# Outputs in the place of inverses, an earlier first state, and a store ahead of the offsets: a chunked RWKV recurrence on one core

## The chip, the cores and the metric

The kernel runs on one core of a Trainium2 chip. The core has five engines that run their own instruction streams and meet through semaphores: TensorE (PE, matrix products; PEld is its weight load), VectorE (DVE), ScalarE (ACT, functions such as exp and ln), GpSimd (POOL) and SyncE (SP), and sixteen DMA engines that move data between the memory of the chip and the on-chip memories: SBUF, and PSUM, where TensorE writes its results. The metric is the time of one execution on the device, in microseconds (us).

## The reference

The reference is the WKV recurrence of RWKV: for each of 16 batches and each of 256 channels a running, exponentially decaying weighted mean of v with weights exp(k), kept stable by a running maximum. k and v have the shape 16 x 2048 x 256 in float32, w and u have 256 elements.

```python
for b in range(batch):
    aa, bb, pp = 0, 0, -1e38                    # per channel
    for t in range(seq_len):
        kk, vv = k[b, t], v[b, t]
        ww = u + kk
        qq = np.maximum(pp, ww)
        e1, e2 = np.exp(pp - qq), np.exp(ww - qq)
        output[b, t] = (e1 * aa + e2 * vv) / (e1 * bb + e2 + 1e-08)
        ww = pp - w + kk
        qq = np.maximum(ww, kk)
        e1, e2 = np.exp(ww - qq), np.exp(kk - qq)
        aa, bb, pp = e1 * aa + e2 * vv, e1 * bb + e2, qq
```

The decay carries the key with it: the new exponent is pp - w + kk, so the exponents are running sums over time, which the kernel builds with triangular matrices.

## The kernel before

Time is cut into 16 chunks of 128 steps, and the 16 batches into 4 groups of 4. A tile is one chunk of one group: 128 time steps (on the partitions) by 4 batches by 256 channels, 512 KB in float32. There are 64 tiles of k and 64 of v, and tile n is group n % 4 of chunk n // 4. The main loop handles one tile of k and v in each pass (a slot, numbered n), and the output of tile q = n - 9 nine slots later (`LAG`), because the state that enters a chunk must first be known. Ten more slots drain the last outputs.

For each tile:

- `round_k`: DVE rounds k for TensorE; `logs`: PE builds the logarithms of the weights in PSUM; `exps`: ACT takes the exponential of both kinds of weights (EZ) in bf16; `cast_v`: v to bf16 (some tiles of v are cast by the transfer itself); `times_v`: DVE multiplies the weights by v.
- `sums`: PE sums the weights, and the weights times v, over half chunks, for the state.
- `den`, `recip`: PE sums the denominators in PSUM, ACT makes their inverse as exp(-ln(x)) in an SBUF tile rd; `num`, `mult`: PE sums the numerators, DVE multiplies them by the inverse; `store`.

```python
    kpool = ctx.enter_context(tc.tile_pool(name="kpool", bufs=AHEAD))      # AHEAD = 6
    vpool = ctx.enter_context(tc.tile_pool(name="vpool", bufs=6))
    vbpool = ctx.enter_context(tc.tile_pool(name="vbpool", bufs=4))
    rpool = ctx.enter_context(tc.tile_pool(name="rpool", bufs=2))
    opool = ctx.enter_context(tc.tile_pool(name="opool", bufs=3))
...
    def recip(n, between=lambda: None):
        rd = rpool.tile([128, 2, D], F32, tag="rd", name="rd")
        for i in (slice(0, 1), slice(1, 2)) if n == NP - 1 else (slice(0, 2),):
            K(SC.activation(rd[:, i, :], DENB[:, i, :], ACT.Ln, scale=RS))
            between()
            K(SC.activation(rd[:, i, :], rd[:, i, :], ACT.Exp, scale=-1.0))
        RD[n] = rd
...
    def mult(n, bank, i):
        if n not in OT:
            OT[n] = opool.tile([128, 4, Dm], F32, tag="ot", name="ot")
        o, rd = OT[n].rearrange("p (i n) d -> p i (n d)", i=2), RD[n]
        K(DVE.tensor_mul(o[:, i, :], bank, rd[:, i, :]))

    def store(n):
        RD.pop(n)
        K(POOL.dma_start(out=rows_of(out, n), in_=OT.pop(n)))
```

Once for each chunk c there is a chain of small operations on the state, spread over the slots after the chunk's last tile by a plan. It ends with four transfers from SP (`inject`) that write the state into a row of the weights, where the denominators and numerators pick it up:

```python
    def state_frames(c):
        E = DVE if c in (0, NST - 1) else POOL
        LL, F = LL_of[c % 2], F_of[c % 2]
        for h, x in enumerate((LL_of[(c + 1) % 2][:, 1, :, 2:3], LL[:, 1, :, 1:2])):
            K(E.tensor_tensor(F[:, :, 1 + h:2 + h], x, LL[:, 1, :, 1 + h:2 + h], ALU.add))
...
    def state_scan(c):
        flat = [x.rearrange("p m s -> p (m s)") for x in (P_of[c % 2], F_of[c % 2], LL_of[c % 2][:, 0])]
        K(DVE.tensor_tensor_scan(*flat, 0.0, ALU.add, ALU.max))

    def state_offsets(c):
        E = DVE if c in (0, NST - 1) else POOL
        A, P, F = [x[c % 2] for x in (A_of, P_of, F_of)]
        Q = tiny.tile([128, 32, 2], F32, tag="Q", name="Q")
        K(E.tensor_tensor(Q, P[:, :, 0:2], F[:, :, 1:3], ALU.add))
        out = A.rearrange("p h m -> p m h")
        K(E.tensor_tensor(out[:, :, 0:2], Q, P[:, :, 1:3], ALU.subtract))
        K(E.tensor_single_scalar(out[:, :, 2:4], Q, CAP, op=ALU.min))
        K(E.tensor_single_scalar(out[:, :, 4:6], P[:, :, 1:3], -1.0, op=ALU.mult))
        K(E.tensor_copy(LL_of[(c + 1) % 2][:, 0, :, 0:1], P[:, :, 2:3]))
...
    def inject(c):
        cb = small.tile([128, 128], BF16, tag="cb", name="cb")
        K(DVE.tensor_copy(cb, st.pop((c, "CT"))))
    ...                                   # four transfers from SP into EZR
...
    later = {}
    for c in range(NST):
        s = 4 * c + 3
        plan = [(s + 1, "act", copy_sums), (s + 1, "pe", turn),
                (s + 2, "act", state_logs), (s + 2, "mid", state_frames), (s + 2, "chain", state_scan), (s + 2, "chain", state_offsets),
                (s + 3, "act", state_weights), (s + 3, "chain", state_chain),
                (s + 4, "nums", turn_back), (s + 4, "mid", inject), (s + 4, "mid", state_next)]
        if c == NST - 1:
            plan = [(s + 1, "copy", copy_sums), (s + 1, "turn", turn),
                    (s + 1, "recip", state_logs), (s + 1, "mid", state_frames), (s + 1, "mid", state_scan), (s + 1, "mid", state_offsets),
                    (s + 2, "recip", state_weights), (s + 2, "mid", state_chain),
                    (s + 3, "turn", turn_back), (s + 3, "first", inject)]
        for slot, where, f in plan:
            later.setdefault((slot, where), []).append((f, c))
```

The loops (the first nine slots, the main slots, the drain):

```python
    for n in range(LAG):

        load(n + AHEAD)
        exps(n)
        logs(n + 1)
        if n and n % 4 == 0:
            sums(n - 1)
        small_work(n, "act")
        small_work(n, "nums")
        if n % 4:
            sums(n - 1)
        small_work(n, "pe")
        idle_matmuls(4, NUMB)
        times_v(n)
        cast_v(n + 1)
        round_k(n + 2)
        small_work(n, "mid")
        small_work(n, "chain")
...
    for n in range(LAG, NP):

        q, qp = n - LAG, n - LAG - 1
        if n + AHEAD < NP:
            load(n + AHEAD)
        first = n == LAG
        if not first:
            num(qp, NUMB, 0)
            den(q)
        if n % 4 == 0:
            sums(n - 1)
        small_work(n, "nums")
        exps(n)
        small_work(n, "act")
        if not first:
            recip(q)
            mult(qp, NUMB, 0)
        small_work(n, "mid")
        if n + 2 < NP:
            round_k(n + 2)
        if n + 1 < NP:
            cast_v(n + 1)
        else:
            times_v(n)
        if not first:
            num(qp, NUMB, 1)
            mult(qp, NUMB, 1)
        small_work(n, "chain")
        if not first:
            store(qp)
        if n + 1 < NP:
            times_v(n)
            logs(n + 1)
        else:
            den(q + 1)
...
    sums(NP - 1)
    small_work(NP, "copy")
    for n in range(NP, NP + LAG + 1):

        q, qp = n - LAG, n - LAG - 1
        H = PS[:, 2 * (n % 2):2 * (n % 2) + 2, :]
        for i in range(2):
            num(qp, H[:, i, :], i)
        small_work(n, "turn")
        small_work(n, "first")
        if q < NP:
            recip(q, lambda: small_work(n, "recip"))
        if q + 1 < NP:
            den(q + 1)
        if qp == NP - 1:
            last_outputs(qp, H)
        else:
            mult(qp, H, slice(0, 2))
            store(qp)
        small_work(n, "mid")
        small_work(n, "pe")
        small_work(n, "last")
    assert not later
```

## Time and profile before

The median of three runs is 308.87 us (308.04 to 309.64). The profiled execution has a span of 307.7 us and a mean granted TensorE clock of 0.991.

| what | value |
|---|---|
| POOL busy | 220.5 us (72%), of which 150 us are the issue of transfers |
| read from HBM, written to HBM | 67.12 MB, 33.55 MB: 327 GB/s over the span |
| issue to landing, median: k, v, v cast to bf16 | 9.4, 9.8, 10.0 us |
| issue to landing, median: outputs, injected states | 8.1, 6.2 us |
| DVE, costliest groups | output multiplication 85.9 us, times v 78.1, rounding of k 48.5, cast of v 40.3 |
| ACT, costliest groups | exponentials of the weights 102.3 + 17.4 us, logarithm and exponential of the inverse 65.3 + 68.0 |
| first and last start of the big exponential (slots 9 and 63) | 38.2 and 275.8 us |

The page of a profile gives each engine's busy time and share of the span, then the span in 40 equal slices (each digit is the busy share in tenths), the DMA queues, the chain of work that ended last, the costliest groups of instructions with what ended the idle time ahead of them, and the transfers. Further views list who waited for whom (`A <- B: us in total, times, longest`) and the instructions of an engine in order of time: start, duration, engine, line, operation, tile written <- tile read, and in brackets the idle time before it and what ended it. Matmuls are pipelined, so a busy PE is not PE at its peak. Line numbers such as L198 are those of the kernel before.

### The profile page before, as it was taken

What the parts mean: (1) busy time and instruction counts of PE and PEld (TensorE: products, weight loads), DVE (VectorE), ACT (ScalarE), POOL (GpSimd) and SP (SyncE); (2) the same over time, 40 slices, a digit from 0 to 9 for tenths busy, and PEclk for the clock granted to TensorE, in tenths of its full rate; (3) what the DMA queues carried; (4) which work ended last, traced back from release to release, by engine and by line L of the source; (5) the groups of instructions that cost most, each with busy time, mean ns of one, the idle gap of its engine ahead of it and who ended that gap; (6) DMA issues with size and microseconds to landing.
All of it is one profiled execution on the core that took longest, in us unless ns stands there. A gap on an engine that the chain in (4) does not pass through costs nothing.

```text
span 307.7 us, 4967 instructions
## 1 busy us (share of the span) xinstructions
PE 274.2 (89%) x1716; PEld 126.6 (41%) x1716; DVE 263.4 (86%) x436; ACT 258.4 (84%) x251; POOL 220.5 (72%) x337
## 2 busy tenths in 40 slices
...
DMA  6999999999999999999989999999999999424676
GB/s 198 349 347 349 334 343 340 366 299 335 367 373 365 280 364 356 363 363 380 305 254 361 360 367 342 349 369 315 361 342 361 360 378 364 153 94 153 215 245 205
DMA packets 37339, 97.86 MB, mean 318 GB/s; under 512 B 6198, under 2 KB 14914, under 8 KB 37314
## 3 DMA queue, kind: packets, MB, share of 16 engines
...
q14 instruction: 12, 0.10, 0.1%
HBM read 67.12 MB, written 33.55 MB: 327 GB/s over the span
## 4 chain that ended last, share of the span: by engine, by line
DMA 27%; DVE 23%; PE 18%; POOL 11%; ACT 10%; issue 8%; DVEq 0%; SPq 0%; POOLq 0%; ACTq 0%
DMA out_dram<-ot 20%; DVE ot L359 7%; PE PS L185 5%; DVE km L171 5%; ACT EZR L198 4%; DMA EZR<-cb 4%; PE PS L353 4%; PE PS L340 4%; ACT rd L346 4%; DVE vb L211 4%; DVE EZR L216 3%; POOL Q L281 3%; DMA kr<-in_k_dram 2%; POOL A L285 2%; PE PS L180 2%
## 5 line engine op out<-in xcount | busy, mean ns | idle before, releaser
L359 DVE TENSOR_TENSOR ot<-PS,rd 128x512 f32<-128x512 f32 (+1 forms) x119 | 85.9, 723 | 24.8 <-PE PS L353 10.1
L198 ACT ACTIVATE EZR<-PS 128x2048 bf16<-128x2048 f32 x55 | 102.3, 1861 | 4.0 <-PE PS L185 3.7
L363 POOL DMA_DIRECT2D out_dram<-ot x63 | 49.5, 786 | 52.7 <-DVE ot L359 50.5
L216 DVE TENSOR_TENSOR EZR<-EZR,vb 128x2048 bf16<-128x2048 bf16 x64 | 78.1, 1220 | 2.3 <-ACT EZR L196 1.8
L346 ACT ACTIVATE rd<-PS 128x1024 f32<-128x1024 f32 (+1 forms) x65 | 65.3, 1005 | 5.6 <-PE PS L340 4.1
L348 ACT ACTIVATE rd<-rd 128x1024 f32<-128x1024 f32 (+1 forms) x65 | 68.0, 1046 | 2.0
L353 PE MATMUL PS<-EZR,LN 128*128 128x512 bf16 x128 | 49.0, 383 | 9.2 <-DVE ot L359 8.9
L63 POOL DMA_DIRECT2D kr<-in_k_dram x63 | 48.6, 772 | 5.9 <-DVE vb L211 2.9
L171 DVE CAST km<-kr 128x1024 fp32r<-128x1024 f32 x64 | 48.5, 757 | 3.4 <-DMA kr<-in_k_dram 3.4
L185 PE MATMUL PS<-km,NLE 128*128 128x512 f32 x128 | 47.4, 452 | 2.3 <-DVE km L171 2.2
L353 PE MATMUL PS<-EZR,IdN 128*128 128x512 bf16 x128 | 48.6, 379 | 0.0
L340 PE MATMUL PS<-EZR,L 128*128 128x512 bf16 x128 | 38.0, 379 | 6.6 <-ACT rd L346 4.0
...
L211 DVE CAST vb<-vr 128x1024 bf16<-128x1024 f32 x50 | 40.3, 805 | 1.3 <-DMA vr<-in_v_dram 1.3
L185 PE MATMUL PS<-km,NLZ 128*128 128x512 f32 x128 | 40.5, 398 | 0.0
L340 PE MATMUL PS<-EZR,Id 128*128 128x512 bf16 x128 | 38.0, 379 | 0.0
L180 PE MATMUL PS<-WU,CO 32*128 32x512 f32 x256 | 33.2, 500 | 3.8 <-ACT EZR L198 3.6
L240 PE MATMUL PS<-EZR,OH 128*32 128x256 bf16 x512 | 25.7, 279 | 1.4 <-DVE tb L299 0.4
L185 PEld LDWEIGHTS PS<-km,NLE 128*128 128x128 f32 x128 | 19.2, 189 | 18.5 <-issue 14.4
L185 PEld LDWEIGHTS PS<-km,NLZ 128*128 128x128 f32 x128 | 24.3, 190 | 5.8
L180 PEld LDWEIGHTS PS<-WU,CO 32*128 32x128 f32 x256 | 12.5, 183 | 32.2 <-ACT EZR L198 17.2
L196 ACT ACTIVATE EZR<-PS 128x1024 bf16<-128x1024 f32 x18 | 17.4, 1020 | 9.9 <-PE PS L185 9.9
...
## 6 DMA issues: line engine op xcount, KB each, us to landing
...
vb<-in_v_dram POOLq DMA_DIRECT2D x14, 256.0 KB, 10.0
EZR<-cb SPq DMA_DIRECT2D x64, 8.0 KB, 6.2
...
```

The source lines that it names most:

```text
L171: K(DVE.tensor_copy(km, kr_of.pop(n)))
L180: K(PE.matmul(half(n, q)[:, i, :], CO[g:g + 32, :], WU[g:g + 32, :], start=True, stop=False, tile_position=(g, 0), skip_group_check=True))
L185: K(PE.matmul(half(n, q)[:, i, :], (NLE, NLZ)[q], km[:, i, :], start=False, stop=True, skip_group_check=True))
L198: K(SC.activation(ez(n)[:, 0:2], PS[:, 0:4, :].rearrange("p (q i) x -> p q i x", q=2), ACT.Exp))
L211: K(DVE.tensor_copy(vb, vr))
L216: K(DVE.tensor_mul(ez(n)[:, 2:4], ez(n)[:, 0:2], vb.unsqueeze(1).broadcast_to([128, 2, 2, D])))
L340: K(PE.matmul(DENB[:, i, :], mats[m], ez(n)[:, q, i, :], start=q == 0, stop=q == 1, skip_group_check=True))
L346: K(SC.activation(rd[:, i, :], DENB[:, i, :], ACT.Ln, scale=RS))
L348: K(SC.activation(rd[:, i, :], rd[:, i, :], ACT.Exp, scale=-1.0))
L353: K(PE.matmul(bank, mats[m], ez(n)[:, q, i, :], start=q == 2, stop=q == 3, skip_group_check=True))
L359: K(DVE.tensor_mul(o[:, i, :], bank, rd[:, i, :]))
L363: K(POOL.dma_start(out=rows_of(out, n), in_=OT.pop(n)))
```

## The change

The change has five parts.

1. **Outputs in the place of inverses.** The multiplication writes its product over the inverse in rd, and the store reads rd. The pool of outputs is gone, rd has six buffers, and v in float32 has five in place of six. It is meant to give a store more time before its buffer is needed again.
2. **Store ahead of the offsets.** In the slot with the scan, POOL issues the store of the slot before it computes the state's offsets, and not after.
3. **Weights amid an inverse.** The state weights G = exp(A) are placed between the logarithm and the exponential of an inverse, and not ahead of both, so that the offsets have longer to come. In the drain the small logs and weights go behind the inverse.
4. **Loads.** SP loads k0, k1 and v0; k is loaded one tile ahead of v in the first slots; the zeros of `wuf` are written by DVE.
5. **An early first state chain.** For chunk 0 the chain is drawn together into two slots, v5 is cast on ACT, and the frames and offsets of chunk 1 run on DVE (as those of chunks 0 and 15 do). The idle products at the start are 12 in place of 16.

The diff (empty lines are cut, marked by dots where more than one):

```diff
--- before.py
+++ after.py
@@ -37,13 +37,13 @@
     LAG = 9
     RS = 2.0 ** -20
     CAP = 54.0
+    ON_DVE = (0, 1, NST - 1)
 
     consts = ctx.enter_context(tc.tile_pool(name="consts", bufs=1))
     kpool = ctx.enter_context(tc.tile_pool(name="kpool", bufs=AHEAD))
-    vpool = ctx.enter_context(tc.tile_pool(name="vpool", bufs=6))
+    vpool = ctx.enter_context(tc.tile_pool(name="vpool", bufs=5))
     vbpool = ctx.enter_context(tc.tile_pool(name="vbpool", bufs=4))
-    rpool = ctx.enter_context(tc.tile_pool(name="rpool", bufs=2))
-    opool = ctx.enter_context(tc.tile_pool(name="opool", bufs=3))
+    rpool = ctx.enter_context(tc.tile_pool(name="rpool", bufs=6))
     small = ctx.enter_context(tc.tile_pool(name="small", bufs=2))
     tiny = ctx.enter_context(tc.tile_pool(name="tiny", bufs=1))
     ps = ctx.enter_context(tc.tile_pool(name="ps", bufs=1, space=bass.MemoryType.PSUM))
@@ -52,7 +52,7 @@
     kr_of, vr_of, VB = {}, {}, {}
 
     def v_mode(n):
-        return "dma" if n >= 9 and n % 4 == 2 else "dve"
+        return "dma" if n >= 9 and n % 4 == 2 else "act" if n in (5,) else "dve"
 
     def rows_of(x, n):
         c, p = divmod(n, 4)
@@ -98,13 +98,14 @@
         K(eng.dma_start(out=wuf.rearrange("(g r) n d -> r g n d", r=32)[r, g0:4], in_=bass.AP(
             tensor=x.tensor, offset=x.offset, ap=[[0, 4 - g0], [0, 2], list(x.ap[0])])))
 
-    K(POOL.memset(wuf, 0.0))
+    fill(wuf, 0.0)
     fill(M1, -1.0)
     fill(I1, 0.0)
     load_k(0, SP)
+    load_k(1, SP)
+    load_v(0, SP)
     load_row(SC, 0, 0, w)
     load_row(SC, 1, 2, u)
-    load_v(0, SC)
     K(SC.preload_act_table_set("natural_log_exp_and_others"))
     fill(idle, 0.0)
     select(M1, GE, 0.0, -1, -1, [[1, 128]])
@@ -114,8 +115,8 @@
                     allow_small_or_imprecise_dtypes=True))
     for g in (2, 3):
         select(COf, NE, 1.0, -32 * g - 1, 1, [[0, 128]])
-    for n in range(1, 3):
-        load(n)
+    load_k(2)
+    load_v(1)

     NLE, NLZ, CO = matrix("NLE", F32R), matrix("NLZ", F32R), matrix("CO", F32R)
@@ -138,7 +139,8 @@
         for h in range(2):
             select(Sel[:, j, h], NE, 1.0, -r - h, 1, [[-16, 2], [-2, 4], [-32, 2]])
     for n in range(3, AHEAD):
-        load(n)
+        load_k(n)
+        load_v(n - 1)
     WU = consts.tile([128, D], F32R, tag="WU", name="WU")
     mats = {"OH": OH, "Sel": Sel.rearrange("p a h n c i -> p (a h) n (c i)")}
 
@@ -265,7 +267,7 @@
 
 
     def state_frames(c):
-        E = DVE if c in (0, NST - 1) else POOL
+        E = DVE if c in ON_DVE else POOL
         LL, F = LL_of[c % 2], F_of[c % 2]
         for h, x in enumerate((LL_of[(c + 1) % 2][:, 1, :, 2:3], LL[:, 1, :, 1:2])):
             K(E.tensor_tensor(F[:, :, 1 + h:2 + h], x, LL[:, 1, :, 1 + h:2 + h], ALU.add))
@@ -274,12 +276,13 @@
...
     def state_offsets(c):
-        E = DVE if c in (0, NST - 1) else POOL
+        E = DVE if c in ON_DVE else POOL
         A, P, F = [x[c % 2] for x in (A_of, P_of, F_of)]
+        out = A.rearrange("p h m -> p m h")
         Q = tiny.tile([128, 32, 2], F32, tag="Q", name="Q")
         K(E.tensor_tensor(Q, P[:, :, 0:2], F[:, :, 1:3], ALU.add))
-        out = A.rearrange("p h m -> p m h")
         K(E.tensor_tensor(out[:, :, 0:2], Q, P[:, :, 1:3], ALU.subtract))
         K(E.tensor_single_scalar(out[:, :, 2:4], Q, CAP, op=ALU.min))
         K(E.tensor_single_scalar(out[:, :, 4:6], P[:, :, 1:3], -1.0, op=ALU.mult))
@@ -332,7 +335,7 @@
                     in_=cb[x:x + 32, :]))
 
 
-    RD, OT = {}, {}
+    RD = {}
 
     def den(n):
         for m, q in (("L", 0), ("Id", 1)):
@@ -353,14 +356,11 @@
             K(PE.matmul(bank, mats[m], ez(n)[:, q, i, :], start=q == 2, stop=q == 3, skip_group_check=True))
 
     def mult(n, bank, i):
-        if n not in OT:
-            OT[n] = opool.tile([128, 4, Dm], F32, tag="ot", name="ot")
-        o, rd = OT[n].rearrange("p (i n) d -> p i (n d)", i=2), RD[n]
-        K(DVE.tensor_mul(o[:, i, :], bank, rd[:, i, :]))
+        rd = RD[n]
+        K(DVE.tensor_mul(rd[:, i, :], bank, rd[:, i, :]))
 
     def store(n):
-        RD.pop(n)
-        K(POOL.dma_start(out=rows_of(out, n), in_=OT.pop(n)))
+        K(POOL.dma_start(out=rows_of(out, n), in_=RD.pop(n).rearrange("p i (n d) -> p (i n) d", n=2)))
 
     def last_outputs(n, H):
         c, p = divmod(n, 4)
@@ -368,19 +368,24 @@
             mult(n, H[:, i, :], i)
             for j, eng in ((0, SP), (1, SC)):
                 b = 4 * p + 2 * i + j
-                K(eng.dma_start(out=out[b, c * TC:(c + 1) * TC, :], in_=OT[n][:, 2 * i + j, :]))
+                K(eng.dma_start(out=out[b, c * TC:(c + 1) * TC, :], in_=RD[n][:, i, Dm * j:Dm * j + Dm]))
 
     later = {}
     for c in range(NST):
         s = 4 * c + 3
         plan = [(s + 1, "act", copy_sums), (s + 1, "pe", turn),
-                (s + 2, "act", state_logs), (s + 2, "mid", state_frames), (s + 2, "chain", state_scan), (s + 2, "chain", state_offsets),
-                (s + 3, "act", state_weights), (s + 3, "chain", state_chain),
+                (s + 2, "act", state_logs), (s + 2, "mid", state_frames), (s + 2, "chain", state_scan), (s + 2, "store", state_offsets),
+                (s + 3, "recip", state_weights), (s + 3, "chain", state_chain),
                 (s + 4, "nums", turn_back), (s + 4, "mid", inject), (s + 4, "mid", state_next)]
+        if c == 0:
+            plan = [(s + 1, "act", copy_sums), (s + 1, "pe", turn), (s + 1, "round", state_logs),
+                    (s + 1, "round", state_frames), (s + 1, "round", state_scan), (s + 1, "round", state_offsets),
+                    (s + 2, "act", state_weights), (s + 2, "chain", state_chain), (s + 2, "chain", turn_back),
+                    (s + 2, "round", inject), (s + 2, "round", state_next)]
         if c == NST - 1:
             plan = [(s + 1, "copy", copy_sums), (s + 1, "turn", turn),
-                    (s + 1, "recip", state_logs), (s + 1, "mid", state_frames), (s + 1, "mid", state_scan), (s + 1, "mid", state_offsets),
-                    (s + 2, "recip", state_weights), (s + 2, "mid", state_chain),
+                    (s + 1, "post", state_logs), (s + 1, "mid", state_frames), (s + 1, "mid", state_scan), (s + 1, "mid", state_offsets),
+                    (s + 2, "post", state_weights), (s + 2, "first", state_chain),
                     (s + 3, "turn", turn_back), (s + 3, "first", inject)]
         for slot, where, f in plan:
             later.setdefault((slot, where), []).append((f, c))
@@ -393,33 +398,37 @@
         for _ in range(n):
             K(PE.matmul(bank, idle[:, 0:128], idle, start=True, stop=True, skip_group_check=True))
 
-    idle_matmuls(16, MISC)
+    idle_matmuls(12, MISC)
     round_k(0)
     K(DVE.tensor_copy(WU, wuf.rearrange("p n d -> p (n d)")))
     logs(0)
+    round_k(1)
     cast_v(0)
-    round_k(1)
     state_start()
     for n in range(LAG):
 
-        load(n + AHEAD)
+        load_v(n + AHEAD - 1)
+        load_k(n + AHEAD)
         exps(n)
-        logs(n + 1)
-        if n and n % 4 == 0:
+        if n % 4 == 0 and n:
             sums(n - 1)
         small_work(n, "act")
-        small_work(n, "nums")
+        if v_mode(n + 1) == "act":
+            cast_v(n + 1)
+        logs(n + 1)
         if n % 4:
             sums(n - 1)
         small_work(n, "pe")
         idle_matmuls(4, NUMB)
         times_v(n)
-        cast_v(n + 1)
+        small_work(n, "chain")
         round_k(n + 2)
-        small_work(n, "mid")
-        small_work(n, "chain")
+        small_work(n, "round")
+        if v_mode(n + 1) != "act":
+            cast_v(n + 1)
         if n == 0:
             out_matrices()
+    load_v(LAG + AHEAD - 1)
     for n in range(LAG, NP):
 
         q, qp = n - LAG, n - LAG - 1
@@ -435,7 +444,7 @@
         exps(n)
         small_work(n, "act")
         if not first:
-            recip(q)
+            recip(q, lambda: small_work(n, "recip"))
             mult(qp, NUMB, 0)
         small_work(n, "mid")
         if n + 2 < NP:
@@ -450,6 +459,7 @@
         small_work(n, "chain")
         if not first:
             store(qp)
+        small_work(n, "store")
         if n + 1 < NP:
             times_v(n)
             logs(n + 1)
@@ -470,19 +480,18 @@
         for i in range(2):
             num(qp, H[:, i, :], i)
         small_work(n, "turn")
-        small_work(n, "first")
         if q < NP:
-            recip(q, lambda: small_work(n, "recip"))
+            recip(q)
+        small_work(n, "post")
         if q + 1 < NP:
             den(q + 1)
+        small_work(n, "first")
         if qp == NP - 1:
             last_outputs(qp, H)
         else:
             mult(qp, H, slice(0, 2))
             store(qp)
         small_work(n, "mid")
-        small_work(n, "pe")
-        small_work(n, "last")
     assert not later
```

## The prediction

> **What bounds the kernel now.** I read the page first: line 2 of it (slices and DMA), then the waits, then the timelines of ACT, DVE and POOL in an ordinary stretch, and last the head of the chain that ended last. A *slot* below is one pass of the loop over n, which handles one tile of k and v; 64 tiles make 64 slots, and ten more slots drain the outputs.
>
> The page says that no engine is alone at the limit. PE, DVE and ACT are all near 90% in the middle, and the DMA engines are full from the second slice to the thirty-fourth and half empty after it:
>
> ```profile
> PE 274.2 (89%) x1716; PEld 126.6 (41%) x1716; DVE 263.4 (86%) x436; ACT 258.4 (84%) x251; POOL 220.5 (72%) x337
> ...
> DMA  6999999999999999999989999999999999424676
> GB/s 198 349 347 349 334 343 340 366 299 335 367 373 365 280 364 356 363 363 380 305 254 361 360 367 342 349 369 315 361 342 361 360 378 364 153 94 153 215 245 205
> ```
>
> So a saving of compute time is worth its full size only where the DMA queue has time in hand. Next the waits, of which these touch the change (columns: who waited for whom, us in total, times, longest):
>
> ```profile
> ACT G L290 <- POOL LL L286: 10.2, 10, 1.2
> DVE ot L359 <- DMA out_dram<-ot: 9.3, 12, 2.5
> POOL Q L281 <- DVE P L275: 8.2, 14, 0.7
> DVE km L171 <- DMA kr<-in_k_dram: 3.4, 4, 1.4
> DVE P L275 <- POOL F L271: 2.3, 1, 2.3
> ```
>
> In the timeline of ACT the loop shows its beat. ACT is busy back to back except ahead of the state weights G:
>
> ```profile
> 58.41 1.86 ACT L198 ACTIVATE EZR<-PS 128x2048 bf16<-128x2048 f32 x1
> 60.16 0.33 ACT L262 ACTIVATE LL<-PS 128x128 f32<-128x128 f32 x1
> 60.33 1.02 ACT L346 ACTIVATE rd<-PS 128x1024 f32<-128x1024 f32 x1
> 61.38 1.06 ACT L348 ACTIVATE rd<-rd 128x1024 f32<-128x1024 f32 x1
> 62.35 1.86 ACT L198 ACTIVATE EZR<-PS 128x2048 bf16<-128x2048 f32 x1
> 65.16 0.36 ACT L290 ACTIVATE G<-A 128x192 f32<-128x192 f32 x1 [0.95 <-POOL LL L286]
> 65.43 1.00 ACT L346 ACTIVATE rd<-PS 128x1024 f32<-128x1024 f32 x1
> 66.47 1.06 ACT L348 ACTIVATE rd<-rd 128x1024 f32<-128x1024 f32 x1
> 67.43 1.86 ACT L198 ACTIVATE EZR<-PS 128x2048 bf16<-128x2048 f32 x1
> ```
>
> From start to start of the big exponential (L198) a plain slot lasts 3.77 us, one with the copy of the sums 4.19, one with LL 3.94 and one with G 5.08: four slots, one chunk of the state, take 17.0 us. Over the whole loop the big exponential of slot 10 starts at 46.43 and that of slot 63 at 275.81, so 53 slots take 229.4 us, 17.3 for four. The 0.3 above the beat are single stalls; the worst, slot 30 to 31 (7.15 us in place of about 4), is this wait for a store, in the timeline of DVE:
>
> ```profile
> 134.06 0.69 DVE L359 TENSOR_TENSOR ot<-PS,rd 128x512 f32<-128x512 f32 x1 [2.51 <-DMA out_dram<-ot]
> ```
>
> At the head the chain waits twice for a transfer: for the second k tile, and for the first injected state, which costs a slot of 8.23 us (38.20 to 46.43):
>
> ```profile
> 3.19 6.24 DMA kr<-in_k_dram
> ...
> 37.19 6.10 DMA EZR<-cb
> ```
>
> **What the Trainium skill says.** (1) "SBUF — State Buffer", section "SBUF: two separate sides": VectorE and GpSimd share a port pair under an exclusive lock, and transfers issued from GpSimd need it for their descriptors. The trace agrees: the same-shaped POOL operations L284 and L285 of the offsets last 438 and 1087 ns in the mean, against 223 and 217 ns on DVE, and a single L285 lasts 0.43 us in one chunk and 1.36 in another. So a later or earlier place of the offsets on POOL is uncertain by some tenths. (2) "DMA: Bandwidth & Descriptors", "Specifications": about 358 GB/s from HBM for one core, 435 GB/s for the fabric. The trace moves 349 in the slices with loads alone and 340 to 380 where loads and stores mix, so the first figure is no hard lid for the mix, but the queue is close to its limit. (3) "ScalarE: Activation LUTs", "What ACT_TABLE_LOAD costs": 186 ns plus 0.833 ns for each element, that is 1039 ns for 1024; the rows of L346 and L348 show 1018 and 1059. A cast of a v tile on ACT should therefore cost about 1.0 us.
>
> **The change, part by part.** I split it into the head (to slot 10), the loop (53 slots) and the drain.
>
> *Head.* k0, k1 and v0 now go out from SP one after another, where k1 waited behind seven constant operations of POOL until 3.19. DVE could round k1 at 9.45 only (1.33 us of waiting, after 1.29 for v0), and ACT stood idle 3.34 us ahead of its first exponentials and 0.92 ahead of the second. k1, issued about 2 us earlier, takes some 1.5 us off. Then k runs one tile ahead of v in the queue; k is needed two slots ahead and v one, so this keeps later slots from stalling; I give it nothing. The first state chain is pulled together: logs, frames, scan and offsets move from slot 5 to slot 4, weights, chain, turn back and injection from slots 6 and 7 to slot 5. The injection is issued two slots (2 x 3.1 us) earlier, at about 28 to 30 in place of 36.5, and has landed at about 36 in place of 43.3. The denominators of tile 0 in slot 9 then find it there. ACT's 4.10 us ahead of the first logarithm (44.41) go, but PE still needs the logs of slot 10 and 1.05 us of denominators, so the slot of 8.23 becomes about 4.5: 3.7 off. Against this stand slot 4, where DVE now waits for ACT's LL with nothing to do, and the cast of v5 on ACT (1.0 us), which takes that time from DVE: about +0.5. The second chunk's frames and offsets (seven small operations of 0.2 us) go to DVE in slot 9, where DVE was idle 2.3 us for POOL: 0.5 to 1 off, which I count against the 0.5. Sum: 1.5 + 3.7 + 0.5 = 5.7 us.
>
> *Loop, the weights.* POOL's offsets run from 61.66 (Q) to 65.1. With the store issued first (0.76 us, the multiplication that it waits for is over at 61.15) Q starts at 61.95 or a little later, so A is there about 0.35 us later, near 65.5. But G now stands between logarithm and exponential: the logarithm starts at 64.1 where the big exponential ends, and is over at 65.15. ACT waits about 0.35 us in place of 0.95 to 1.2. The slot with G falls from 5.08 to about 4.4, and four slots from 17.0 to 16.35. DVE pays a part back: its chain (L298) stood at 65.56 without a gap and would now find G at about 65.85, 0.3 us for four slots; counted by starts, its work is about 16 us for four slots, so it stands at 16.3 too.
>
> *Loop, the buffers.* Outputs had three buffers: the first half of tile q+3 waited for the store of tile q, 2.7 slots or 11 us after its issue, and landings take up to 11.1 us. With six rd tiles the logarithm of q+6 waits for the store of q, which gives five slots, some 20 us. The 9.3 us of DVE waits go. Their worth is the excess over the beat, 17.3 - 17.0 for four slots, 4 us over the loop. The size in place is the same: six rd for three ot and two rd is one tile more, and vr gives one tile (five for six). Of six consecutive v tiles at least one goes straight to bf16 later on, so five vr are enough.
>
> *Loop, the limit of the DMA queue.* Four slots move eleven transfers of 524 KB (one of v counts as 262 KB in bf16) and 33 KB of states: 6.06 MB. In the windows of 8 us from 160 to 256 the mean is 354 GB/s, 17.1 us for four slots, the beat that compute set; in good windows it is 365 to 375, 16.2 to 16.6 us. So the queue gives way to about 16.5, and compute wants 16.35. With the two so close I take 16.85 for four slots, not the sum of both savings: 53/4 x 16.85 = 223.3, against 229.4: 6.2 us off.
>
> *Drain.* ACT sets it: 2.13 us for logarithm and exponential of each tile. Its small logs and weights waited inside this pair, 0.91 us for PE and 0.27 for DVE, and 0.87 us were spent on an rd buffer. All three go by moving them behind the exponential and by more buffers; the later chain stalls PE's turn back by up to 0.8. 1.0 us off.
>
> Sum: 308.9 - 5.7 - 6.2 - 1.0 = 296.0 us.
>
> **The rivals.** *The queue was the bound all along.* Its shares of 1.0 and more from 8 to 262 speak for it: a faster compute would then only wait for k in place of a store. Against it: the last k tile was issued at 250.0 and landed about ten us later, but was rounded at 268.7, so loads were ahead of compute by some 8 us at the end, and loads waited for cost DVE only 4.7 us in all. Under this rival only the earlier start and the drain count, and the stores that slip ahead of the last loads: 303 to 306 us. *Compute keeps everything.* The queue holds 9 us of backlog and a k tile has 16 us from issue to use, so the difference of 0.2 us for four slots may never be felt. Then the loop runs at 16.4 (217.3 us) and the sum is 290. *The late offsets bite.* If POOL's lock makes store and offsets longer by a us and G is awaited as long as before, now with an idle DVE chain behind it, the loop keeps its 17.0 to 17.3: 299 to 302.
>
> **Range and chances.** The head is visible in the trace and little disputed (5 to 7 us with the drain at least). The loop is open between 0 and 12. I hold 290 to 302. Faster by over 2% means under 302.7: 0.88; within 2%: 0.10; slower: 0.02.
>
> **What would show it.** Right: the wait of DVE for out_dram gone; the one of ACT's G under 0.5 us a time; the injection landing before 38 and the first logarithm of rd without a wait of 4 us; the big exponential of slot 10 at 40 to 41.5; the slots repeating at 16.4 to 16.9 for four; the pure ACT beat of 2.13 in the drain. Wrong: DVE waiting for kr or vr by more than 8 us in all (then the queue is the bound), ACT waiting at G for POOL as before, or a wait of ACT's logarithm for a store (six buffers too few).

## The result and the profile after

| | before | after |
|---|---|---|
| time, median of four runs, us | 309.25 (308.04 to 309.80) | 305.26 (304.80 to 305.49) |
| ratio of after to before | | 0.9874, 95% interval 0.9840 to 0.9909 |
| span of the profiled run, us | 307.7 | 303.8 |
| head: start of the big exponential of slot 9 / 10 | 38.20 / 46.43 | 39.27 / 45.76 |
| loop: from there to that of slot 63 | 229.38 | 226.02 |
| drain: from slot 63 to the end of the span | 31.9 | 32.0 |

The change makes the kernel 4.0 us faster. Of the 12.9 us predicted, the head gave 0.7 in place of 5.7, the loop 3.4 in place of 6.2, and the drain nothing in place of 1.0. These parts come from one profile of each kernel. Three more kernels with the loop of after (e1, e2 and e5 below) take 5.4, 4.0 and 4.4 us less for it than before, so the loop's share is known to a few us only.

The page of after, parts 1 and 2 (busy time by engine; then the slices of about 7.6 us):

```profile
PE 272.0 (90%) x1680; PEld 127.2 (42%) x1712; DVE 267.2 (88%) x443; ACT 259.6 (85%) x252; POOL 211.5 (70%) x328
...
PEclk9699999999999999999999999999999999999997
DMA  7999999999999999999999999999999999244576
GB/s 239 348 348 349 330 346 336 351 322 352 365 364 348 337 361 344 378 337 362 341 347 357 337 367 367 371 352 326 360 357 357 347 363 356 96 165 147 176 270 209
```

PE, DVE and ACT still stand at 85 to 90%. The DMA row is full to the thirty-fourth slice, as before. New is the 6 in the second slice of PEclk. The waits of after (who waited for whom, us in total, times, longest):

```profile
DVE rd L360 <- PE PS L356: 9.0, 13, 2.0
...
ACT EZR L200 <- PE PS L187: 6.1, 14, 1.1
...
DVE WU L403 <- DMA wuf<-in_u_dram: 2.2, 1, 2.2
...
ACT G L293 <- POOL LL L289: 2.0, 8, 0.3
...
ACT G L293 <- POOL A L288: 1.9, 4, 0.7
...
DVE km L173 <- DMA kr<-in_k_dram: 1.2, 1, 1.2
```

Of the two waits that the change was made for, that of DVE for a store is gone (9.3 us before, no such line now), and that of ACT at G has shrunk (10.2 us for LL before; now 2.0 for LL and 1.9 for A, 0.25 and 0.48 us a time in the mean). In their place stands a line that was 3.7 us in 3 waits before and is 6.1 us in 14 now: the big exponential waiting for the logs of PE. The timeline of ACT shows where:

```profile
217.15 1.86 ACT L200 ACTIVATE EZR<-PS 128x2048 bf16<-128x2048 f32 x1
218.91 1.02 ACT L349 ACTIVATE rd<-PS 128x1024 f32<-128x1024 f32 x1
220.18 0.36 ACT L293 ACTIVATE G<-A 128x192 f32<-128x192 f32 x1 [0.25 <-POOL LL L289]
220.45 1.05 ACT L351 ACTIVATE rd<-rd 128x1024 f32<-128x1024 f32 x1
221.40 1.85 ACT L200 ACTIVATE EZR<-PS 128x2048 bf16<-128x2048 f32 x1
223.15 1.01 ACT L349 ACTIVATE rd<-PS 128x1024 f32<-128x1024 f32 x1
224.20 1.06 ACT L351 ACTIVATE rd<-rd 128x1024 f32<-128x1024 f32 x1
225.64 1.88 ACT L200 ACTIVATE EZR<-PS 128x2048 bf16<-128x2048 f32 x1 [0.38 <-PE PS L187]
```

The slot with G (217.15 to 221.40) fell from about 5.1 to 4.25 us. The plain slot behind it, which held no wait before, rose from 3.77 to 4.24. The slot with the copy of the sums went from 4.18 to 4.38. ACT's wait was shared out, not removed. Four slots together, in the stretch of eight from slot 48 to 56, are one row of the windows view each (length, then busy PE, PEld, DVE, ACT, POOL with counts, granted clock, DMA share, GB/s). Before:

```profile
211.46:245.51 34.05, 32.30 (x212) 15.14 (x208) 32.26 (x51) 31.76 (x31) 28.07 (x43) 1.00 1.05 356
```

After:

```profile
208.51:242.63 34.12, 31.99 (x208) 15.08 (x212) 32.45 (x52) 32.11 (x30) 27.25 (x42) 1.00 1.05 359
```

17.03 us for four slots before and 17.06 after: in this stretch the beat did not change. Taken in groups of four slots from 12 to 60, before has none under 16.98 us; after runs from 16.76 to 17.48, and e1, e2 and e5 start at 16.74 to 16.79. So of the 0.65 us that the weights were to give, 0.25 is seen at most, and in single groups only. The 3.4 us of the loop are mostly single stalls. Against a beat of 17.0, the 48 slots from 12 to 60 ran 4.95 us over before (slot 30 alone was 7.15 us long) and 1.65 us over after.

### The profile page after: what moved, and what is told of

It reads as the page before. It is cut to its first block, busy times and chain, and to the rows that moved or that the text cites. A ratio compares the mean times of both kernels' runs of the same rounds, so it can differ in the third digit from the quotient of the medians.

```text
span 303.8 us, 4937 instructions
## 1 busy us (share of the span) xinstructions
PE 272.0 (90%) x1680; PEld 127.2 (42%) x1712; DVE 267.2 (88%) x443; ACT 259.6 (85%) x252; POOL 211.5 (70%) x328
## 3 DMA queue, kind: packets, MB, share of 16 engines
q1 hardware_dynamic: 4944, 2.36, 3.0%
## 4 chain that ended last, share of the span: by engine, by line
PE 39%; DMA 24%; DVE 20%; ACT 10%; issue 4%; SPq 1%; DVEq 0%; POOL 0%; POOLq 0%; ACTq 0%
DMA EZR<-cb 11%; PE PS L187 11%; DMA out_dram<-rd 11%; PE PS L343 8%; PE PS L356 8%; DVE rd L360 6%; DVE EZR L218 5%; PE PS L242 4%; PE PS L182 4%; ACT rd L349 4%; ACT rd L351 3%; DVE km L173 3%; DVE vb L213 3%; PE PS L399 2%; DMA wuf<-in_u_dram 2%
## 5 line engine op out<-in xcount | busy, mean ns | idle before, releaser
L360 DVE TENSOR_TENSOR rd<-PS,rd 128x512 f32<-128x512 f32 (+1 forms) x119 | 85.7, 722 | 15.8 <-PE PS L356 9.0
L363 POOL DMA_DIRECT2D out_dram<-rd x63 | 48.7, 773 | 67.2 <-ACT rd L351 28.4
L356 PE MATMUL PS<-EZR,LN 128*128 128x512 bf16 x126 | 48.2, 382 | 6.1 <-DVE rd L360 6.1
L173 DVE CAST km<-kr 128x1024 fp32r<-128x1024 f32 x64 | 52.5, 820 | 1.2 <-DMA kr<-in_k_dram 1.2
L343 PE MATMUL PS<-EZR,L 128*128 128x512 bf16 x127 | 37.8, 379 | 9.5 <-DMA EZR<-cb 5.4
L71 POOL DMA_DIRECT2D vr<-in_v_dram x49 | 40.2, 820 | 7.2 <-DVE vb L213 5.6
L213 DVE CAST vb<-vr 128x1024 bf16<-128x1024 f32 x49 | 39.0, 795 | 0.0
L356 PE MATMUL PS<-EZR,IdN 128*128 128x512 bf16 x102 | 38.6, 379 | 0.2 <-issue 0.2
L343 PE MATMUL PS<-EZR,Id 128*128 128x512 bf16 x128 | 38.1, 379 | 0.1
L182 PE MATMUL PS<-WU,CO 32*128 32x512 f32 x256 | 33.8, 505 | 2.9 <-DVE WU L403 1.8
L198 ACT ACTIVATE EZR<-PS 128x1024 bf16<-128x1024 f32 x18 | 17.4, 1020 | 13.0 <-PE PS L187 12.9
L182 PEld LDWEIGHTS PS<-WU,CO 32*128 32x128 f32 x256 | 12.9, 185 | 30.5 <-issue 9.1
```

The source lines that it names most:

```text
L173: K(DVE.tensor_copy(km, kr_of.pop(n)))
L182: K(PE.matmul(half(n, q)[:, i, :], CO[g:g + 32, :], WU[g:g + 32, :], start=True, stop=False, tile_position=(g, 0), skip_group_check=True))
L343: K(PE.matmul(DENB[:, i, :], mats[m], ez(n)[:, q, i, :], start=q == 0, stop=q == 1, skip_group_check=True))
L356: K(PE.matmul(bank, mats[m], ez(n)[:, q, i, :], start=q == 2, stop=q == 3, skip_group_check=True))
L360: K(DVE.tensor_mul(rd[:, i, :], bank, rd[:, i, :]))
L363: K(POOL.dma_start(out=rows_of(out, n), in_=RD.pop(n).rearrange("p i (n d) -> p (i n) d", n=2)))
```

## The theories and the runs

For the loop: *DVE theory* (V in the expectations): DVE already set the beat of 17.0, and G's wait was only where ACT paid for it. *Queue theory* (Q; the first rival of the prediction): the transfers set it. *Coupling theory* (B): PE, DVE and ACT are all nearly full and wait for one another, so a wait taken from one comes back at another. For the head: *clock theory* (C): half clock after the new pause of PE costs the start; *loads theory*: loads reach the first slots no sooner, whatever PE does; *order theory* (S): the first denominators stand too late in PE's order.

All times below are medians with their range. Each ratio is to the kernel before as it ran beside that run, where its median was 310.19 us for e1 to e4, 308.29 for e5 to e8, 308.61 for e9 to e12 and 309.99 for e13 and e14. So the medians of different groups are compared by these ratios; that of after is 0.9874. "Loop" is the time from slot 12 to slot 60 divided by twelve, thus for four slots. The same loop code in after, e1, e2 and e5 gives 17.14, 16.97, 17.09 and 17.02, so a single profile's loop figure is good to about 0.15.

| run | us | ratio to before (95%) | slot 10 | loop |
|---|---|---|---|---|
| e1, 16 idle products | 302.48 (301.36 to 304.31) | 0.9754 (0.9689 to 0.9819) | 44.06 | 16.97 |
| e2, rows first | 303.43 (302.39 to 303.97) | 0.9775 (0.9721 to 0.9829) | 44.47 | 17.09 |
| e3, half the mult | 297.37 (295.73 to 298.36) | 0.9578 (0.9518 to 0.9638) | 45.72 | 16.45 |
| e4, half the store | 302.51 (298.44 to 303.07) | 0.9687 (0.9576 to 0.9797) | 45.66 | 16.86 |
| e5, e1 and early denominators | 300.43 (299.96 to 300.95) | 0.9747 (0.9725 to 0.9769) | 41.43 | 17.02 |
| e6, store from SP | 314.16 (313.29 to 318.67) | 1.0179 (1.0146 to 1.0212) | 45.77 | 17.88 |
| e7, more v cast by transfers | 301.72 (301.27 to 304.15) | 0.9804 (0.9762 to 0.9847) | 45.75 | 17.07 |
| e8, before with the buffers alone | 307.75 (305.79 to 310.43) | 0.9968 (0.9935 to 1.0001) | 46.68 | 17.29 |
| e9, after without the new plan | 307.30 (304.62 to 310.00) | 0.9947 (0.9911 to 0.9984) | 45.68 | 17.28 |
| e10, half the num | 305.03 (302.89 to 306.07) | 0.9899 (0.9840 to 0.9958) | 45.58 | 16.97 |
| e11, half an exponential | 303.19 (302.20 to 304.19) | 0.9828 (0.9777 to 0.9880) | 43.65 | 17.08 |
| e12, k from SP | 305.65 (302.78 to 309.37) | 0.9876 (0.9847 to 0.9905) | 43.76 | 17.46 |
| e13, a dose for DVE | 309.68 (307.88 to 313.81) | 1.0009 (0.9980 to 1.0038) | 45.85 | 17.39 |
| e14, a dose for ACT | 304.64 (302.69 to 308.23) | 0.9796 (0.9686 to 0.9907) | 44.79 | 17.13 |

## Experiments on the head

**e1: no pause for PE at the start.** Four more idle products bridge the wait.

```diff
-    idle_matmuls(12, MISC)
+    idle_matmuls(16, MISC)
```

> The changed kernel with 16 idle products at the start in place of 12, nothing else. Theory C (the clock): the products end at about 8.4 us in place of 6.66, TensorE never stands idle, and its clock stays at 1.0 where it was at 0.5 from 10 to 16 us; the first products of the logs still begin at about 8.5, but the first two slots lose about 2 us less: the exponential of slot 10 at about 43.8 in place of 45.76, total 1.5 to 2 us less. Rival N (nothing kept): the head gets shorter, but the loop makes up for it by waiting for loads: total within 0.5 us of the changed kernel.

The timeline of after shows what it is aimed at:

```profile
2.07 4.59 PE L399 MATMUL PS<-CB 128*128 128x512 bf16 x12 [2.07 <-DVE CB L83]
...
7.90 0.50 DVE L403 CAST WU<-wuf 128x512 fp32r<-128x512 f32 x1 [2.19 <-DMA wuf<-in_u_dram]
...
8.46 0.51 PE L182 MATMUL PS<-WU,CO 32*128 32x512 f32 x4 [1.79 <-DVE WU L403]
```

The rows w and u now go out behind k0, k1 and v0, and the weights WU are cast at 7.90, where before they were at 5.53. PE has run out of its twelve idle products and pauses 1.79 us. Then the clock falls; the windows row of after for 10 to 12 us, its third number from the end being the clock:

```profile
10.00:12.00 2.00, 2.00 (x7) 0.90 (x6) 0.69 (x8) 1.81 (x2) 2.00 (x4) 0.50 1.04 350
```

and of e1 for the same stretch:

```profile
10.00:12.00 2.00, 1.79 (x8) 1.04 (x8) 0.84 (x8) 1.67 (x3) 2.00 (x4) 1.00 1.04 352
```

In after the clock is 0.50 from 10 to 16 us, 6.8 us in all with the parts beside; before it was 1.00 there. With 16 products it stays 1.00, though the first logs start no sooner (8.53). Slot 10 comes 1.70 us earlier. The page "TensorE: Matmul & The Clock Gate" of the Trainium skill, section "What's actually happening", tells of halving after an idle window of about 3.4 us; here a pause of 1.79 us was followed by it. By the ratios the whole gains 1.2%, some 3.7 us; where the part beyond the 1.7 lies isn't known.

It is the clock that costs, and not the pause. In e12, with the head of after, PE pauses too, but the clock stays at 1.00:

```profile
2.08 5.02 PE L399 MATMUL PS<-CB 128*128 128x512 bf16 x12 [2.08 <-DVE CB L83]
8.47 0.51 PE L182 MATMUL PS<-WU,CO 32*128 32x512 f32 x4 [1.38 <-DVE WU L403]
...
10.00:12.00 2.00, 1.78 (x9) 1.05 (x8) 0.90 (x8) 1.66 (x3) 2.00 (x4) 1.00 1.02 346
```

Its slot 10 starts at 43.76, sooner than that of e1. The same twelve products last 4.06 to 5.30 us in the runs with this head, so the pause behind them differs: with 1.79 us or more (after, e3, e4, e6, e7, e9, e10, e13) the clock is always 0.50 for 6.8 us; with 1.38 (e11, e12) there is no dip; but e14, with 1.09, has one of 3.4 us. The length of the pause alone does not decide it.

**e2: the rows first.** k1 and v0 move behind the rows, onto ACT's queue.

```diff
-    load_k(1, SP)
-    load_v(0, SP)
     load_row(SC, 0, 0, w)
     load_row(SC, 1, 2, u)
+    load_k(1, SC)
+    load_v(0, SC)
```

> The changed kernel with the second k tile and the first v tile issued from ACT behind the rows of w and u, and not from SP ahead of them; SP loads the first k alone. Theory R (the rows): the small loads of w and u land at about 5.5 in place of 7.84, as in the kernel before, so the wait of 2.19 us ahead of WU goes, the idle products join up with the logs, the clock stays at 1.0 and the first exponential starts at about 8.0 in place of 9.88. By slot 10 it is 4 us earlier (near 42), and the total 3 to 4 us less. Rival N: the loop gives it back to loads, total within 1 us of the changed kernel.

The first exponential starts at 8.13 in place of 9.88, and yet slot 10 gains only 1.29 us, less than e1, which started its exponentials at 9.72. So the early start, with the clock at 1.00 throughout, bought no more than e1 did with a late one: DVE now waits 4.7 us in three waits for k in place of 1.2 in one, as the loads theory says. The half clock cost the head 1.3 to 2.0 us (e2, e1, e12), and e2 does not get beyond that, where slot 10 near 42 was expected.

**e5: the first denominators ahead of the logs of slot 10.** On top of e1.

```diff
         small_work(n, "nums")
+        if first:
+            den(q)
         exps(n)
         small_work(n, "act")
+        if first:
+            recip(q)
 ...
-        if first:
-            den(q)
-            recip(q)
```

> The run with 16 idle products, and in slot 9 the first denominators and the first inverse ahead of the logs of slot 10 and not behind them. Theory S (the slot of 6.49 us between the first two big exponentials is a chain through PSUM: exponential, logs of the next slot, denominators, logarithm, exponential): the denominators run while the exponential does, the slot falls to about 4.3, so about 2 us come off the run with 16 idle products alone. Rival I (the injected state was still awaited): the denominators can not start earlier, and nothing changes.

The timeline of after between the two big exponentials of slots 9 and 10 (ACT, and two rows of PE):

```profile
39.27 1.88 ACT L200 ACTIVATE EZR<-PS 128x2048 bf16<-128x2048 f32 x1 [1.12 <-PE PS L187]
...
41.20 0.50 PE L182 MATMUL PS<-WU,CO 32*128 32x512 f32 x4 [0.69 <-ACT EZR L200]
...
42.66 0.61 PE L343 MATMUL PS<-EZR,L 128*128 128x512 bf16 x2
...
43.74 1.02 ACT L349 ACTIVATE rd<-PS 128x1024 f32<-128x1024 f32 x1 [2.36 <-PE PS L343]
44.80 1.06 ACT L351 ACTIVATE rd<-rd 128x1024 f32<-128x1024 f32 x1
45.76 1.86 ACT L200 ACTIVATE EZR<-PS 128x2048 bf16<-128x2048 f32 x1
```

The injection is issued at 32.02 (36.53 before), and no product waits for it here. But the logs of slot 10 (L182) wait for the exponential of slot 9 to empty their half of PSUM, the denominators (L343) stand behind them, and the logarithm waits 2.36 us for these. In e5:

```profile
37.26 1.88 ACT L200 ACTIVATE EZR<-PS 128x2048 bf16<-128x2048 f32 x1 [1.12 <-PE PS L187]
39.04 0.34 ACT L264 ACTIVATE LL<-PS 128x128 f32<-128x128 f32 x1
39.41 1.03 ACT L349 ACTIVATE rd<-PS 128x1024 f32<-128x1024 f32 x1
40.46 1.06 ACT L351 ACTIVATE rd<-rd 128x1024 f32<-128x1024 f32 x1
41.43 1.86 ACT L200 ACTIVATE EZR<-PS 128x2048 bf16<-128x2048 f32 x1
```

The slot takes 4.17 us in place of 6.49, and slot 10 starts 2.63 us earlier than in e1. That is the order theory. How much of it reaches the end is not shown: the ratios of e5 and e1, 0.9747 and 0.9754, can't be told apart, and e5's profile is 1.0 us longer from slot 10 to 63. These two are the fastest versions that compute everything, and by their ratios faster than both kernels.

## Experiments on the loop

**e3: less work for DVE.** In the main loop the multiplication takes half of its elements only; half of the outputs of these tiles stay inverses.

```diff
-        K(DVE.tensor_mul(rd[:, i, :], bank, rd[:, i, :]))
+        if isinstance(i, int) and n < NP - LAG - 1:
+            K(DVE.tensor_mul(rd[:, i, 0:Dm], bank[:, 0:Dm], rd[:, i, 0:Dm]))
...
```

> The changed kernel with only half of the columns of each output multiplied in the main loop (the other half is stored as inverses, so the output leaves work out); transfers are as before. Theory V (VectorE sets the beat): it loses 8 x 0.27 us in four slots, the beat of 17.0 us for four slots falls to the next limit, about 16.2 to 16.6 (ACT's own work is 16.0), so the loop of 53 slots gets 6 to 10 us shorter and DVE shows waits again. Theory Q (the DMA queue sets the beat): the beat stays within 0.1 us, and DVE waits for loads or ACT for DVE's input.

The eight slots from 48 to 56 in the windows view of e3:

```profile
201.90:234.73 32.83, 31.60 (x208) 14.96 (x212) 27.47 (x51) 32.02 (x30) 30.51 (x43) 1.00 1.05 367
```

The beat falls from 17.06 to 16.42 for four, with all transfers at their full size: 367 GB/s in place of 359. So the queue does not set 17.0. DVE lost about 2.5 us for four slots and the beat 0.65, because ACT takes over: 32.02 busy of 32.83, with 0.40 us idle where after has 1.66. POOL, too, fits its issues and offsets into the shorter beat. The slots are now 4.38, 4.1, 3.97 and 3.97 us.

**e10 and e11: less work for PE, and for ACT.** e10 leaves out one of the two products of each numerator, e11 half of the exponentials of the inverses (outputs without these parts), both in the main loop.

```diff
+            if n < NP - LAG - 1 and q == 3:
+                continue
...
```

> The changed kernel with one of the two products of each numerator left out in the main loop (so the output leaves that term out): PE loses 8 x 0.22 = 1.7 us in four slots, nothing else changes. Theory B: PE's share gets idle, the beat falls by 0.2 to 0.6 of these 1.7 us. Theory PE (PE alone sets the beat): it falls by 1.0 or more. Theory V (DVE alone): it stays within 0.1.

```diff
-            K(SC.activation(rd[:, i, :], rd[:, i, :], ACT.Exp, scale=-1.0))
+            h = slice(0, 1) if n < NP - LAG - 1 else i
+            K(SC.activation(rd[:, h, :], rd[:, h, :], ACT.Exp, scale=-1.0))
```

> The changed kernel with the second function of the inverse taken over half of the columns in the main loop (the other half stays a logarithm, so the output leaves that out): ACT loses 4 x 0.43 = 1.7 us in four slots, nothing else changes. Theory B: the beat falls by 0.2 to 0.6 us. Theory V or theory PE: it stays within 0.1.

In the stretch of slots 48 to 56 PE's busy time falls by 3.05 us in e10 and ACT's by 2.87 in e11, and the loop stays at 16.97 and 17.08. That is inside the spread of unchanged loops: neither sets the beat alone. Slot by slot PE does matter: in e10 the slot with the copy of the sums falls from 4.38 to about 4.17 and the one behind G from 4.24 to about 4.02, but the two others take it back. In e11 the freed time returns at once: ACT's wait for the logs of PE is 18.8 us in place of 6.1. The lower total of e11 comes mostly from the head (slot 10 at 43.65).

**e13 and e14: more work for DVE, and for ACT.** One more small operation in every main slot: a fill on DVE, 0.193 us from start to start, and a copy on ACT, 0.216.

```diff
         small_work(n, "store")
+        fill(dose, 0.0)
```

> The changed kernel with one more write of zeros to an unused 128x256 tile by DVE in every slot of the main loop, about 0.24 us each, so some 1 us in four slots. Theory V (DVE sets the beat): the beat of 17.1 us for four slots rises by 0.7 to 1.0, the total by 9 to 12 us. Theory B (PE, DVE and ACT share the beat): by 0.2 to 0.5, 3 to 6 us.

```diff
+        K(SC.activation(dose[:, 0:128], dose[:, 128:256], ACT.Copy))
```

> The changed kernel with one more copy of an unused 128x128 tile by ACT in every slot of the main loop, about 0.2 us each, so some 0.8 us in four slots. Theory V: ACT has about 0.9 us of idle time in four slots and takes it from there; the beat rises by less than 0.2, the total by less than 2.5 us. Theory B: by 0.2 to 0.5, 3 to 6 us, as for DVE.

The windows of slots 48 to 56, of e13:

```profile
210.97:245.76 34.79, 31.96 (x208) 15.05 (x212) 33.39 (x59) 31.93 (x30) 28.12 (x42) 1.00 1.05 351
```

and of e14:

```profile
207.28:241.40 34.12, 32.17 (x208) 15.06 (x212) 32.72 (x51) 33.26 (x39) 28.16 (x42) 1.00 1.06 358
```

The dose of 0.77 us for four slots on DVE makes the beat 0.33 longer, and the ratio to before goes from 0.9874 to 1.0009, some 4.2 us. The dose of 0.86 on ACT leaves the beat of this stretch as it was: ACT is now busy 33.26 of 34.12 us and the four slots are still 17.06. That speaks for the DVE theory and against ACT; with e10, PE is out as well. But neither theory held as it was written. The DVE theory said 0.7 to 1.0 for DVE's dose, and 0.33 lies in the range of the coupling theory, which in turn said 0.2 to 0.5 for ACT's dose and 0.2 to 0.6 for the relief of PE and ACT. Only a part of DVE's dose is felt: its casts become shorter (the rounding of k takes 0.67 us from start to start in place of 0.78), about 0.4 us for four slots. Its idle time in the stretch, 0.98 us, tells nothing, as the same loop has 1.54 in after and 0.51, 0.42 and 1.06 in e1, e2 and e5.

**e4, e6 and e12: who issues the transfers.** e4 stores half of each output tile; e6 lets SP issue the stores and e12 the loads of k, both with all bytes.

```diff
-        K(POOL.dma_start(out=rows_of(out, n), in_=...))
+        h = 2 if n < NP - LAG - 1 else 4
+        K(POOL.dma_start(out=rows_of(out, n)[:, 0:h], in_=...[:, 0:h]))
```

> The changed kernel with only two of four batches stored for each tile of the main loop (half of each output is left out); the work of all engines but the issue of stores is the same. Theory V: the beat stays at 17.0 us for four slots, total within 1 us. Theory Q: the queue loses 4 x 262 KB of 6.06 MB in four slots, a sixth, and the beat falls to ACT's and DVE's limit, 16.2 to 16.5: 6 to 10 us less.

```diff
-        K(POOL.dma_start(out=rows_of(out, n), in_=...))
+        K((SP if n < NP - LAG - 1 else POOL).dma_start(out=rows_of(out, n), in_=...))
```

> The changed kernel with the stores of the main loop issued from SP and not from POOL; bytes and all work of the compute engines are the same. Theory P (VectorE sets the beat, and its casts are stretched while POOL writes the descriptors of transfers): DVE's rounding of k falls from a mean step of 0.78 to about 0.65 us, the beat from 17.1 to 16.6 us for four slots, the total by 4 to 6 us. Rival W (the work of DVE is what it is, the casts are long for another reason): the beat stays within 0.1. Rival Q (transfers): stores from SP go out in smaller packets, the queue gets slower and the beat longer.

```diff
-            load(n + AHEAD)
+            load_k(n + AHEAD, SP)
+            load_v(n + AHEAD)
```

> The changed kernel with the loads of k in the main loop issued from SP, where nothing queues for long, and the stores on POOL as they are. Theory P (POOL's writing of descriptors stretches DVE's casts, and this is part of the beat): DVE's rounding of k falls from a mean step of 0.78 to 0.68 us, the beat to about 16.6 for four slots (as it was between the stalls of the run with stores from SP), and without that run's stalls the total is 4 to 6 us less. Rival Q (transfers in packets of 1 KB are slower): DVE waits for k, and the total is not below that of the changed kernel.

Why the issuer matters is seen in DVE's timeline of after: the same cast of k, once at 210.24 and once at 218.66, each with the operation that follows it:

```profile
210.24 0.98 DVE L173 CAST km<-kr 128x1024 fp32r<-128x1024 f32 x1
211.14 0.87 DVE L213 CAST vb<-vr 128x1024 bf16<-128x1024 f32 x1
...
218.66 0.68 DVE L173 CAST km<-kr 128x1024 fp32r<-128x1024 f32 x1
219.25 0.73 DVE L213 CAST vb<-vr 128x1024 bf16<-128x1024 f32 x1
```

From start to start it takes 0.90 us the first time and 0.59 the second. At 209.95 and 210.69 POOL issues transfers; from 217.34 to 220.05 it does none. Over the 37 k tiles of slots between 100 and 260 us, the ten casts with next to no transfer issue beside them take 0.60 us in the mean, the 27 with one 0.84; for v it is 0.67 and 0.80. At 27 of 37 and 13 of 28 this makes 4 x 0.24 x 27/37 + 3 x 0.13 x 13/28, about 0.9 us of DVE's time for four slots. The page "SBUF — State Buffer" of the Trainium skill, section "Who interferes with whom", has those casts of DVE that run in a two-port mode and the descriptor writes of GpSimd on one lock, where the other side fully blocks; the trace agrees that they collide, and shows the cost to DVE as 0.24 us of a cast, not as the whole 0.75 us of an issue. With the k loads on SP, the windows of e12 give

```profile
210.85:243.88 33.03, 31.97 (x208) 15.18 (x211) 31.31 (x51) 31.68 (x31) 19.63 (x34) 1.00 1.03 346
```

DVE's busy time falls by 1.14 us for eight slots, and the beat by 1.09, to 16.52 for four: nearly one for one. Of e12's twelve groups of four slots, five take 16.49 to 16.66 us, three 17.07 to 17.13, and four hold stalls; after has none under 16.76. The kernel moves all its bytes, but in this stretch at 346 GB/s, 11.4 MB of the 12.1 that eight slots need, so the stretch lived in part on tiles loaded before. (The profiled execution of e12 was longer than most of its timed ones, so its stretches are read, and not its whole.) e4 and e6 show the same between their stalls: 16.56 to 16.76.

Neither e6 nor e12 is a gain, and the waits of e6 say why:

```profile
PEld L343 <- DMA EZR<-cb: 16.1, 8, 3.0
...
PE PS L343 <- DMA EZR<-cb: 8.8, 7, 2.6
```

The denominators wait for the four injected state transfers of 8 KB, which SP also issues: they now queue behind 512 KB of stores or k. Slots of 7.4 and 7.8 us appear in e6 and one of 7.85 in e12, where PE waits 2.66 us for the state. The page "DMA: Bandwidth & Descriptors", section "Queues, rings and completion order", says that a ring's descriptors are consumed in order; the trace agrees (in after these waits are 6.4 us for the weight loads, none over 1.4, and 5.4 for the products, none over 0.9; in e12 13.1 and 9.2 us, up to 3.1 and 2.7). e4, which has less to move on the queue as well, cannot part the two causes; e12 can.

**e7: casts moved from DVE to the transfers.** Every second v tile instead of every fourth is cast by its load (four v buffers, seven for bf16).

```diff
-        return "dma" if n >= 9 and n % 4 == 2 else "act" if n in (5,) else "dve"
+        return "dma" if n >= 9 and n % 2 == 0 else "act" if n in (5,) else "dve"
```

> The changed kernel with every second tile of v cast to bf16 by its transfer (every fourth before), seven buffers for it and four for float32. DVE has one cast of about 0.74 us less in four slots; the transfer queue has more to do (a cast tile takes it longer than a plain one, though it writes half the bytes). Theory V: the beat falls from 17.1 to about 16.4 for four slots, 7 to 9 us less in all. Theory Q: the queue pays, the beat stays or gets longer, and DVE waits for k or v.

DVE is freed of one cast, about 0.74 us for four slots, and the loop comes out at 17.07, in the spread of unchanged loops. DVE's idle time in the stretch grows from 1.54 to 2.49 us. The DVE theory said 16.4 here, so this is a miss. From slot 48 on the slots take 4.38, 4.01, 4.26 and 4.22 us, as in after, the relieved one (the last) too: something other than DVE's work sets its length, and what it is was not tested. The ratio of 0.9804 lies below after's 0.9874 with intervals that just meet; the profile does not show where, and I leave that open.

**e8 and e9: which part gave the loop's 3.4 us.** e8 is the kernel before with six rd tiles and five vr and nothing else; e9 is after with offsets and weights at their old places.

```diff
-    vpool = ctx.enter_context(tc.tile_pool(name="vpool", bufs=6))
+    vpool = ctx.enter_context(tc.tile_pool(name="vpool", bufs=5))
-    rpool = ctx.enter_context(tc.tile_pool(name="rpool", bufs=2))
-    opool = ctx.enter_context(tc.tile_pool(name="opool", bufs=3))
+    rpool = ctx.enter_context(tc.tile_pool(name="rpool", bufs=6))
```

> The kernel before with the first part of the change alone: products in the place of inverses, six rd, five vr. Theory V: the plain beat of 17.0 us for four slots stays, and the single stalls ahead of a product (a slot of 7.15 us, some of 0.3 to 0.9) go: 3 to 4 us less than before, nearly the whole gain of the changed kernel. Rival G (the gain of the changed kernel comes from the weights between logarithm and exponential): within 1 us of the kernel before.

```diff
-                (s + 2, "act", state_logs), ..., (s + 2, "store", state_offsets),
-                (s + 3, "recip", state_weights), ...
+                (s + 2, "act", state_logs), ..., (s + 2, "chain", state_offsets),
+                (s + 3, "act", state_weights), ...
```

> The changed kernel with two of its parts undone in the loop: POOL computes the offsets ahead of the store, and the state weights stand ahead of both halves of an inverse, as before. Theory B (PE, DVE and ACT are all filled to about 95% of the beat and wait for one another, so that a wait taken from one comes back at another): ACT waits for POOL's LL by 10 us again, the beat stays at 17.0 to 17.1 us for four slots, total within 1.5 us of the changed kernel. Rival G (the weights and the store ahead brought the gain of the loop): 3 us more than the changed kernel.

e8: no DVE wait for a store, slot 30 falls from 7.15 to 5.10, but slots of 5.63, 5.03 and 5.30 stand elsewhere: 1.4 us off the 48 slots, and a ratio of 0.9968 whose interval holds 1, where 3 to 4 us were expected. e9: G waits 10.9 us for POOL again, and 48 slots take 1.7 us longer than in after; its ratio is 0.9947, some 2.3 us more than after's 0.9874. The 1.4 and the 1.7 us are no more than equal loops differ by (0.15 for four slots is 1.8 for 48), so how the loop's gain is split stays open; the ratios show a gain for the plan and none for the buffers alone. In e9's undisturbed slots (3.77, 4.2, 3.95, 5.1) four make 17.0, the fixed pattern of before.

## Why the prediction was wrong, by its own steps

*Head, the second k tile ("takes some 1.5 us off"): lost.* k1 was rounded at 8.32 in place of 9.45, but the rows it now precedes came later, PE paused, and the clock halved. Slot 9 started 1.07 us later than before. I had counted nothing for the rows or for the clock. With the clock at 1.00 slot 9 starts at 37.57 (e1) and 37.25 (e12), 0.6 to 0.95 us earlier than before; for the rest of the 1.5, e2 points to the loads.

*Head, "the slot of 8.23 becomes about 4.5": this step failed.* The injection came early, though not at 28 to 30: it was issued at 32.02. But "PE still needs the logs of slot 10 and 1.05 us of denominators" left out that these logs wait for the exponential of slot 9 and stand ahead of the denominators, so ACT's own 1.88 us lie in series with them, and then 2.1 us of inverse ahead of the next exponential. It became 6.49. With the order turned, in e5, it is 4.17.

*Loop, the weights: the mechanism was right, the consequence wrong.* G waits 0.25 to 0.48 us a time (0.35 predicted), and its slot is 4.25 (4.4 predicted). The step that failed is "counted by starts, its work is about 16 us for four slots, so it stands at 16.3 too". Over slots 12 to 60, DVE's work from start to start, its idle gaps taken out, was 16.25 us for four slots before, 16.39 after, and 16.42 to 16.52 in e1, e2 and e5. It grew with the rounding of k, whose mean step went from 0.71 us to 0.76 to 0.80. And 0.44 to 0.75 us of gaps came on top in these four profiles, where the step had taken the rest for free time. The beat answers DVE's work (e3, e12 and e13, but not e7), and relief of PE or ACT did not shorten it measurably. About 0.9 us of DVE's own sum is its collision with POOL's transfer issues, which the prediction saw on POOL's operations only. ACT's wait at G did fall, from 0.88 to 0.33 us for four slots, but ACT waited for PE's logs instead.

That DVE set the 17.0 of before as well is not shown, since no run changed the work of one engine there. In the same stretch of before DVE waits three times for a store, and the slots keep their 3.95, 5.11 and 5.14 us, so it had some time in hand:

```profile
216.40 0.69 DVE L359 TENSOR_TENSOR ot<-PS,rd 128x512 f32<-128x512 f32 x1 [0.40 <-DMA out_dram<-ot]
220.29 0.69 DVE L359 TENSOR_TENSOR ot<-PS,rd 128x512 f32<-128x512 f32 x1 [0.40 <-DMA out_dram<-ot]
237.34 0.69 DVE L359 TENSOR_TENSOR ot<-PS,rd 128x512 f32<-128x512 f32 x1 [0.43 <-DMA out_dram<-ot]
```

*Loop, the buffers ("4 us over the loop"): right in kind.* The 9.3 us of waits are gone, and the excess over the beat fell by 3.3 us. But e8 gives the buffers alone only 1.4 of these, no more than equal loops differ by: its slots no longer wait for a store, but stall for POOL ahead of G (1.50 us in slot 14) or for PE (slot 33).

*Loop, the queue ("gives way to about 16.5"): not the bound at 17.0.* e3 runs at 16.42 with every byte, and e12 at 16.5 in its best groups. What the queue would allow below this was not tested. (53/4 x 16.85 us takes 6.1 off the 229.4, not 6.2.) The rival in which the queue was the bound all along named the right range (303 to 306) for the wrong cause: its sign, over 8 us of DVE waiting for loads, stayed away at 1.2. "Compute keeps everything" fell with the 16.4 it needs. "The late offsets bite" did not come about: G waits 3.9 us in all.

*Drain ("all three go"): they moved.* The three waits it named, 0.91, 0.27 and 0.87 us, are gone, and three others stand in ACT's timeline of after:

```profile
278.49 1.02 ACT L349 ACTIVATE rd<-PS 128x1024 f32<-128x1024 f32 x1 [0.46 <-PE PS L343]
...
283.47 1.02 ACT L349 ACTIVATE rd<-PS 128x1024 f32<-128x1024 f32 x1 [0.62 <-PE PS L343]
...
288.83 1.02 ACT L349 ACTIVATE rd<-PS 128x1024 f32<-128x1024 f32 x1 [1.11 <-PE PS L343]
```

2.19 us in place of 2.05. PE had itself waited 0.72 us for the state at its turn back (282.17) and 1.34 us ahead of the denominators at 287.77, 1.44 us after the last state injection had been issued (283.61 to 286.33). So it seems to be the last chunk's chain that sets these, and moving it behind the exponentials made it later, as the prediction feared with "up to 0.8". I read this from the traces alone; no run tested it.

The range of 290 to 302 took the head as "visible in the trace and little disputed". It was the larger miss, 5.0 us; the loop missed 2.8 (0.8 to 2.2 in e1, e2 and e5, with the same loop) and the drain 1.1.

Open: what holds DVE idle for 0.44 to 0.75 us in four slots; what set the beat before; why a pause of 1.38 us passes without a dip of the clock and one of 1.09 does not; and a version that has SP issue loads with the injections on a ring of their own, which would show whether 16.5 lasts. It wasn't tried.
